# Rotation tables a layer early, a norm on VectorE alone, and other buffer counts in a two-block transformer kernel on one core

## The chip, the cores and the metric

The kernel runs on one core of a Trainium2 chip. The metric is the device time of one execution in microseconds (us), as the median of several runs. In the profile PE is TensorE's matmul stream and PEld its weight loads, DVE is VectorE, ACT is ScalarE, POOL is GpSimd, and SP (SyncE) issues most of the DMAs.

## The reference

The input is one sequence of 512 tokens of width 1024. The first block is two hybrid layers, each a mixer (sparse attention, gated linear attention, pooling) and a convolutional gated feed-forward part, and it ends with a norm. The second block has four layers that run over 256 context tokens and the 512 latent tokens; each is a gated mixer on a normalised and modulated stream, without a feed-forward part. Layers 0 and 3 are of kind 0 (grouped-query attention with axial rotation), layer 1 is of kind 1 (neighbourhood attention) and layer 2 of kind 2 (differential attention, with rotation). What matters here:

```python
# end of the first block: x = rms_norm(x, final_norm_g)

def mixer_a(u, uc, q_g, k_g, ang, need_ctx):       # kind 0
    def heads(t):
        q, k, v = jnp.split(t, [q_dim, q_dim + kv_dim], axis=-1)
        q = rms_norm_2(q.reshape(b, n, A_KV_HEADS, A_GROUP, HEAD_DIM), q_g)
        k = rms_norm_2(k.reshape(b, n, A_KV_HEADS, HEAD_DIM), k_g)
        return q, k, v.reshape(b, n, A_KV_HEADS, HEAD_DIM)
    q, k, v = heads(u)
    qc, kc, vc = heads(uc)
    q, k = axial_rope(q, ang), axial_rope(k, ang)
    o = gqa_attention(q, jnp.concatenate([kc, k], axis=1), jnp.concatenate([vc, v], axis=1))
    ...

def _rotate(x, ang):
    x1, x2 = jnp.split(x, 2, axis=-1)
    ...
    return jnp.concatenate([x1 * cos - x2 * sin, x2 * cos + x1 * sin], axis=-1)
```

The gains q_g and k_g can be multiplied into the cosines and sines, since they depend on the layer and the head's element only. That product is what the kernel calls the rotation tables.

## The kernel before

All products that need float32 precision are made of float16 pairs: a value is split into a high half (ACT casts it) and a low half (POOL or DVE subtracts), and three matmuls add hi by hi, lo by hi and hi by lo. Projections run in units of 128 output columns and two tiles of 128 tokens: 48 matmuls of 128x256 fill one of the two PSUM banks named pj (lines 1609 to 1611). The weights come by DMA as wst and are split into whi (line 376) and wlo (line 377).

The program is a set of Python generators, one for projections and one for attention, that yield after each piece of work. A timeline scheduler then sets the final order of the instructions of each engine by estimated times, and places tiles. So a small edit moves instructions far away from it. Each engine runs its own list in order; POOL also issues the small loads of constants, SP the weight loads and the transposing DMAs.

At the seam of the blocks `first_norm` makes the row scales of the final norm as a PSUM tile px (named bx in the trace). From it `make_h` makes the first layer's normalised stream hh and hl (for the latents) without waiting for x itself; then `scale` multiplies x by px and the gain in place, for the eight pieces of 128 channels.

`mixer(i)` runs one layer of the second block. It loads gains and rotation angles (POOL's DMA queue) and makes the tables rc2 and rs2 on POOL. Then follow the jobs of the heads. A job fills the u tile (128 tokens x 6 token tiles x 128 columns) from pj by ACT (line 1626), squares it, and reduces the squares on DVE (line 1629). Together with a query's columns the gate's columns sz are made from the same bank: ACT's tanh (1792) and DVE's product (1793), which is the bank's last reader; for a key it is the value's remainder vl (1691). When u is full, POOL makes the inverse root qny (421), DVE scales u by it (1658), `rope` makes four products f with rs2 (1651) and one with rc2 (1653) on POOL and adds them on DVE (1654). A query then goes through `put_query`: ACT casts it to qst, POOL makes the remainder (1668), SP transposes it to qs. A key goes through `put_key` with the two tiles kst and klt in the same way (1681, 1682, 1685).

Attention takes scores S from PSUM, DVE finds the negative maximum nm (698), ACT makes P by the exponential (701), ACT casts P to hl (717), POOL makes the remainder (718), SP transposes hl to pt, and PE multiplies with the values (728 to 730). The tiles hl, kst and klt of kind 0 share a ring of four buffers (tag phl). The result of a head pair is split into ohl by ACT (1811) and DVE (1812), and a transposing DMA brings it to og, the left operand of the output projection in `out_pair` (392 to 394 are its matmuls).

Of the kernel before, what the change touches and what calls it, by code (L numbers as in the profile page):

```python
# [8 lines left out]
F32 = mybir.dt.float32  # L9
F16 = mybir.dt.float16  # L10
# [3 lines left out]
OP = mybir.AluOpType  # L14
# [4 lines left out]
S = 512  # L19
# [10 lines left out]
GK = 32.0  # L30
# [187 lines left out]
class Kern:  # L218
# [205 lines left out]
    def setup(self):  # L424
        nc, I, const = self.nc, self.I, self.const
# [30 lines left out]
        self.mod = const.tile([128, 4, 24, 2], F32, name="mod")  # L456
        self.adas = self.ada()
        self.nada = self.nmod = 0

# [216 lines left out]
    def expo(self, su, q, segs, mask=None, bias=None, add=None):  # L676
# [14 lines left out]
        p = self.pp.tile([128, self.wide], F32, name="P", tag="P", bufs=self.nbuf[0])  # L691
        nm = self.sm.tile([128, 1], F32, name="nm")
        if bias is None:
# [8 lines left out]
        else:  # L702
            mx = self.sm.tile([128, 1], F32, name="mx")
            nc.vector.tensor_reduce(mx, s[:, 256:512], axis=AX.X, op=OP.min)
            nc.vector.tensor_tensor_reduce(out=p[:, :256], in0=s[:, :256], in1=bias, op0=OP.add, op1=OP.min,
                                           scale=1.0, scalar=mx, accum_out=nm)
            s2 = self.sm.tile([128, 2], F32, name="su2")
            nc.scalar.activation(p[:, :256], p[:, :256], AF.Exp, bias=nm, scale=-1.0, accum_out=s2[:, 0:1])
# [90 lines left out]
    def mixers1(self, l):  # L799
# [144 lines left out]
        def attn(c, qs, kh, kl, vh, vl):  # L944
            for t in range(4):
# [3 lines left out]
                for h in range(2):  # L949
# [4 lines left out]
                    def second(t=t, h=h, pt=pt, su=su):  # L954
# [5 lines left out]
                        if h:  # L960
                            ri = self.sm.tile([128, 2], F32, name="ri")
                            nc.vector.reciprocal(ri, su)
# [331 lines left out]
    def context(self):  # L1294
# [23 lines left out]
        self.lam()  # L1318
        yield True
        self.norm_h(acc, self.vec, CTX, 1.0)  # L1320
        for _ in range(8):
            yield True

    def first_norm(self, accs):
# [4 lines left out]
        a = self.sm.tile([128, 8], F32, name="ag")  # L1329
        nc.vector.tensor_tensor(a, self.vec[0][:, 0], g, op=OP.mult)  # L1330

        def chain(ms):
# [19 lines left out]
            def scale():  # L1352
                for c in range(KD):
                    t = self.f()
                    nc.vector.tensor_scalar(t, px, g[:, c:c + 1], 1.0 / GK, op0=OP.mult, op1=OP.mult)
                    nc.gpsimd.tensor_tensor(self.x[:, c], self.x[:, c], t, op=OP.mult)
                self.dump("xf", self.x)
# [98 lines left out]
    def spare(self, limit):  # L1456

        while self.nada < limit:
            next(self.adas, None)
            yield True  # L1460

    def mixer(self, i):
        nc, I = self.nc, self.I
        kind, j, need = i % 3, i // 3, i < 3
        with ExitStack() as es:
            self.pl = self.pool("pl", 2, es=es)
            pl = self.pl
            G = self.vec[2]
            gv = pl.tile([128, 4, 64], F32, name="gv", bufs=1) if kind == 1 else self.f(256).rearrange("p (a d) -> p a d", a=4)
            nc.gpsimd.dma_start(gv.rearrange("p a d -> p (a d)"), I["gqk"][i:i + 1].to_broadcast([128, 256]))  # L1470
            if kind != 1:

                self.rc2 = pl.tile([128, 2, 6, 64], F32, name="rc2", bufs=1)
                self.rs2 = pl.tile([128, 2, 4, 64], F32, name="rs2", bufs=1)
                rot = self.f().rearrange("p (a t d) -> p a t d", a=2, t=4)
                nc.gpsimd.dma_start(rot, I["rot"].rearrange("p (a t d) -> p a t d", a=2, t=4))
                for t, r, g in ((self.rc2[:, :, 0:4], rot[:, 0], 0), (self.rs2, rot[:, 1], 2)):
                    nc.gpsimd.tensor_tensor(t, r.unsqueeze(1).to_broadcast([128, 2, 4, 64]),
                                            gv[:, g:g + 2].unsqueeze(2).to_broadcast([128, 2, 4, 64]), op=OP.mult)
                nc.gpsimd.tensor_copy(self.rc2[:, :, 4:6], gv[:, 0:2].unsqueeze(2).to_broadcast([128, 2, 2, 64]))  # L1480
            else:
                self.bm = pl.tile([128, 4, 4, 8], F32, name="bm", bufs=1)
                nc.gpsimd.dma_start(self.bm, I["bm"].rearrange("p (j m c) -> p j m c", j=4, m=4))
                self.gg2 = gv[:, 0]
                nc.vector.scalar_tensor_tensor(gv[:, 0], gv[:, 0], -0.125, gv[:, 1], op0=OP.mult, op1=OP.mult)
# [72 lines left out]
    def out_pair(self, p, G, need, i):  # L1558
# [11 lines left out]
        if final and need:  # L1570
            v = self.vec = self.vectors(i + 1)
            self.ready = set()
        for n in ((CTX,) if need else ()) + ((LAT0, LAT1) if final else (LAT,)):
            while final and self.done[n] < 8:
# [42 lines left out]
    def heads(self, n4, then):  # L1617
# [4 lines left out]
        def done(ps, t):  # L1622
            if not got:
                got.extend((self.pl.tile([128, 6, 128], F32, name="u", bufs=2), self.sm.tile([128, 6, 2], F32, name="qss", bufs=4)))
            u, ss = got[:2]
# [35 lines left out]
    def put_query(self, u, n4, qs):  # L1661

        nc = self.nc
        st = self.pl.tile([128, 2, 6, 2, 64], F16, name="qst", tag="stg", bufs=(1,2,2)[self.kind])[:, :, :n4]
        s = st.rearrange("p h t e d -> p t h e d")
# [132 lines left out]
    def attn_group(self, i, kind, g, need, st):  # L1798
# [7 lines left out]
        def put_og(os, t):  # L1806

            if g < (6,6,6,0)[i]:
                for k, o in enumerate(os):
                    v = pl.tile([128, 256], F16, name="ohl", bufs=2)  # L1810
                    nc.scalar.activation(v[:, :128], o, AF.Copy, scale=0.5 * WI)
# [49 lines left out]
        for t in tiles:  # L1861
            cs = []
            su = self.sm.tile([128, 2], F32, name="su", bufs=6)
            for h in range(2):
# [29 lines left out]
                if kind != 2:  # L1894
                    pt = self.item(su[:, h:h + 1], q, segs, bias=bias)

                    def second(t=t, h=h, pt=pt, su=su, vb=vb):
                        c = slice(64 * h, 64 * h + 64)
                        if h == 0:
                            self.o = self.psO()[:, :128]  # L1900
                            ri = self.sm.tile([128, 2], F32, name="ri")
                            nc.vector.reciprocal(ri, su)
# [66 lines left out]
```

## Time and profile before

| quantity | us |
|---|---|
| median of three runs (2887.4, 2887.79, 2878.65) | 2887.4 |
| profiled execution | 2885.51 |
| its span, first to last instruction | 2883.7 |
| TensorE matmuls busy | 2609.6 |
| DVE busy | 2027.3 |
| ACT busy | 1633.9 |
| POOL busy | 1528.1 |

Times in the rows count from the first instruction of the profiled execution. The second block begins near 1290; its layers begin near 1290, 1690, 2090 and 2590. A timeline row gives start and duration, the engine, the line of the kernel, the operation, the tiles that are written and read, and in square brackets how long the engine was idle before it and what ended that. A window row gives for a stretch the busy time of every engine with the count of its instructions, then the mean granted TensorE clock (1.00 is 2.4 GHz, 0.50 is 1.2 GHz), the share of the DMA engines and their rate.

### The profile page before, as it was taken

Reading aid. Unit: us, or ns where it says so; the run is one execution under the profiler, and the core shown is the slowest. Engines: PE = TensorE matmul, PEld = TensorE weight load, DVE = VectorE, ACT = ScalarE, POOL = GpSimd, SP = SyncE. Lnnn points to the kernel's source line nnn. Section 1 sums busy time; section 2 is a strip of 40 time slices with the busy share of each in tenths; the row PEclk is TensorE's granted clock in tenths of the full one; section 3 lists DMA queues with packets and bytes.
Section 4 is the critical chain, followed back from the end, with each engine's and each line's share of the span. In section 5 each row is a group of like instructions: output and inputs, shape, how many; then the busy total and the mean of one; then the engine's idle time right before and its main releaser. Section 6 shows DMA issues by size and latency. Waiting matters only on the chain. (4 is left out here: it accounts for less than half of the span.)

```text
span 2883.7 us, 58883 instructions
## 1 busy us (share of the span) xinstructions
PE 2609.6 (90%) x22594; PEld 1755.9 (61%) x22604; DVE 2027.3 (70%) x3731; ACT 1633.9 (57%) x3471; POOL 1528.1 (53%) x1341
## 2 busy tenths in 40 slices
PE   7899999999889999998988889999879998978896
PEld 4564444445554444447766678887668786657764
DVE  5966787536966888436767677666668888686775
ACT  6575555335575655333775656665545665455773
POOL 6773222116763432216786647776555555345984
PEclk8999999999999999999999999999999999989999
DMA  4346565333355565332799727887525555423995
GB/s 157 101 105 157 176 198 191 106 104 93 105 126 157 165 205 190 100 105 70 149 165 178 140 77 149 168 167 156 112 62 112 115 119 119 99 61 95 193 188 110
DMA packets 645165, 385.24 MB, mean 134 GB/s; under 512 B 564511, under 2 KB 574545, under 8 KB 644881
## 3 DMA queue, kind: packets, MB, share of 16 engines
q1 hardware_dynamic: 643328, 378.39, 54.7%
q8 instruction: 177, 2.90, 0.4%
q0 software_dynamic: 1120, 2.88, 0.4%
q14 instruction: 108, 0.88, 0.1%
q10 hardware_dynamic: 432, 0.20, 0.0%
HBM read 232.71 MB, written 2.10 MB: 81 GB/s over the span
## 5 line engine op out<-in xcount | busy, mean ns | idle before, releaser
L718 POOL TENSOR_TENSOR hl<-P,hl 128x768 f16<-128x768 f32 (+4 forms) x368 | 463.9, 1267 | 247.9 <-ACT hl L717 205.7
L377 DVE SCALAR_TENSOR_TENSOR wlo<-wst,whi 128x1024 f16<-128x1024 f32 (+1 forms) x292 | 377.6, 1294 | 234.2 <-ACT whi L376 233.1
L1609 PE MATMUL pj<-whi,hh 128*128 128x256 f16 x1664 | 458.0, 276 | 28.1 <-DVE vl L1691 14.3
L1610 PE MATMUL pj<-wlo,hh 128*128 128x256 f16 x1664 | 457.7, 275 | 0.0
L1611 PE MATMUL pj<-whi,hl 128*128 128x256 f16 x1664 | 456.1, 275 | 1.8 <-DVE hl L1452 1.7
L376 ACT ACTIVATE whi<-wst 128x1024 f16<-128x1024 f32 (+1 forms) x292 | 304.4, 1045 | 263.9 <-PE pj L393 149.7
L701 ACT ACTIVATE P<-S,nm 128x768 f32<-128x768 f32 (+4 forms) x352 | 250.9, 715 | 178.0 <-DVE nm L698 91.0
L393 PEld LDWEIGHTS <-whi 128*128 128x128 f16 x1936 | 191.0, 99 | 224.1 <-issue 45.1
L392 PEld LDWEIGHTS <-whi 128*128 128x128 f16 x1936 | 191.3, 99 | 207.6 <-issue 17.1
L394 PEld LDWEIGHTS <-wlo 128*128 128x128 f16 x1936 | 191.1, 99 | 194.9 <-issue 7.2
L717 ACT CAST hl<-P 128x768 f16<-128x768 f32 (+4 forms) x368 | 231.5, 637 | 78.6 <-DMA pt<-hl 45.3
L698 DVE TENSOR_REDUCE nm<-S 128x1 f32<-128x768 f32 (+4 forms) x320 | 236.1, 749 | 48.1 <-PE S L686 34.0
L685 PE MATMUL S<-kh,qs 128*128 128x256 f16 (+3 forms) x672 | 203.0, 310 | 48.2 <-ACT P L701 27.1
L728 PE MATMUL O<-vh,pt 128*128 128x64 f16 (+1 forms) x1472 | 189.5, 200 | 53.7 <-DMA pt<-hl 46.8
L1609 PE MATMUL pj<-whi,mxl 128*128 128x256 f16 x704 | 196.3, 279 | 21.2 <-DVE sz L1793 11.5
L1610 PE MATMUL pj<-wlo,mxl 128*128 128x256 f16 x704 | 196.3, 279 | 1.5 <-DVE wlo L377 1.5
L1611 PE MATMUL pj<-whi,mxl 128*128 128x256 f16 x704 | 195.0, 278 | 1.8 <-DVE mxl L1452 1.8
L686 PE MATMUL S<-kl,qs 128*128 128x256 f16 (+3 forms) x672 | 193.7, 311 | 0.0
L421 POOL TENSOR_TENSOR qny<-qss,mhalf 128x12 f32<-128x12 f32 (+1 forms) x52 | 130.2, 2504 | 118.9 <-DVE qss L1635 114.3
L728 PEld LDWEIGHTS <-pt 128*128 128x128 f16 x1536 | 143.5, 99 | 75.7 <-DMA pt<-hl 66.6
L729 PE MATMUL O<-vl,pt 128*128 128x64 f16 (+1 forms) x1472 | 188.7, 200 | 0.0
L730 PE MATMUL O<-vh,pt 128*128 128x64 f16 (+1 forms) x1472 | 188.1, 200 | 0.0
(398 smaller groups left out, 7697.1 us busy)
## 6 DMA issues: line engine op xcount, KB each, us to landing
wst<-i_wts SPq DMA_DIRECT2D x318, 512.0 KB
ast<-i_ada_w SPq DMA_DIRECT2D x96, 512.0 KB
wst<-i_wts SPq DMA_DIRECT2D x16, 384.0 KB
pt<-hl SPq DMA_TRANSPOSE x368
rpb<-i_rpb SPq DMA_DIRECT2D x8, 384.0 KB
xin<-i_x SPq DMA_DIRECT2D x4, 512.0 KB
kh<-h SPq DMA_DIRECT2D x32, 64.0 KB
kl<-h SPq DMA_DIRECT2D x32, 64.0 KB
```

The source lines that it names most:

```text
L376: nc.scalar.activation(hi[:, :n], st[:, :n], AF.Copy, scale=s)
L377: nc.vector.scalar_tensor_tensor(lo[:, :n], st[:, :n], s, hi[:, :n], op0=OP.mult, op1=OP.subtract)
L685: nc.tensor.matmul(d, q, kh, start=True, stop=False)
L686: last = nc.tensor.matmul(d, q, kl, start=False, stop=(mask is None))
L698: nc.vector.tensor_reduce(nm, s[:, :w], axis=AX.X, op=OP.max, negate=True)
L701: nc.scalar.activation(p[:, :w], s[:, :w], AF.Exp, bias=nm, scale=-1.0 if neg else 1.0, accum_out=su)
L717: nc.scalar.copy(hl[:, :w], p[:, :w])
L718: nc.gpsimd.tensor_tensor(hl[:, w:2 * w], p[:, :w], hl[:, :w], op=OP.subtract)
L728: nc.tensor.matmul(o, pt[:, i], vh, start=(i == 0), stop=False)
L1609: nc.tensor.matmul(d, hh[:, k, s], hi[:, k % 4], start=(k == 0), stop=False)
L1610: nc.tensor.matmul(d, hh[:, k, s], lo[:, k % 4], start=False, stop=False)
L1611: nc.tensor.matmul(d, hl[:, k, s], hi[:, k % 4], start=False, stop=(k == KD - 1))
```

## The change

- The tables rc2 and rs2 become tiles that live through the second block. A new function `tables(i)` loads gains and angles and makes them: for layer 0 within the context generator, which runs beside the last feed-forward part of the first block; for layers 2 and 3 in the final `out_pair` of the layer before. `mixer` itself only loads what kind 1 needs.
- In `first_norm`, `scale` was eight DVE products into a temporary and eight POOL products into x. Now it is eight DVE instructions that read px, a scaled gain gs and x, and write x.
- Buffers: u has 3 instead of 2 in kind 0. nm, mx, su2 and ri have 4 instead of 2. ohl has 4 instead of 2. qst, which in kind 0 had one buffer of its own (tag stg), now takes one of the ring of four (tag phl); in kinds 1 and 2 it stays where it was.
- The space for descriptors of POOL's DMAs is 1024 instead of 2048 bytes a partition.

```diff
@@ __init__
+        self.rc2 = const.tile([128, 2, 6, 64], F32, name="rc2")
+        self.rs2 = const.tile([128, 2, 4, 64], F32, name="rs2")
@@ expo (the same for mx, su2; ri in two more places)
-        nm = self.sm.tile([128, 1], F32, name="nm")
+        nm = self.sm.tile([128, 1], F32, name="nm", bufs=4)
@@ context
+        self.tables(0, self.pf)
+        yield True
@@ first_norm
+        gs = self.sm.tile([128, 8], F32, name="gs", bufs=1)
+        nc.vector.tensor_scalar_mul(gs, g, 1.0 / GK)
...
-                    t = self.f()
-                    nc.vector.tensor_scalar(t, px, g[:, c:c + 1], 1.0 / GK, op0=OP.mult, op1=OP.mult)
-                    nc.gpsimd.tensor_tensor(self.x[:, c], self.x[:, c], t, op=OP.mult)
+                    nc.vector.scalar_tensor_tensor(self.x[:, c], px, gs[:, c:c + 1], self.x[:, c], op0=OP.mult, op1=OP.mult)
@@ new
+    def tables(self, i, tmp=None):
+        nc, I = self.nc, self.I
+        gv, rot = (tmp.tile([128, n], F32, name=f"rt{n}", bufs=1) for n in (256, S)) if tmp else (self.f(256), self.f())
+        gv = gv.rearrange("p (a d) -> p a d", a=4)
+        nc.gpsimd.dma_start(gv.rearrange("p a d -> p (a d)"), I["gqk"][i:i + 1].to_broadcast([128, 256]))
+        rot = rot.rearrange("p (a t d) -> p a t d", a=2, t=4)
+        nc.gpsimd.dma_start(rot, I["rot"].rearrange("p (a t d) -> p a t d", a=2, t=4))
+        for t, r, g in ((self.rc2[:, :, 0:4], rot[:, 0], 0), (self.rs2, rot[:, 1], 2)):
+            nc.gpsimd.tensor_tensor(t, r.unsqueeze(1).to_broadcast([128, 2, 4, 64]),
+                                    gv[:, g:g + 2].unsqueeze(2).to_broadcast([128, 2, 4, 64]), op=OP.mult)
+        nc.gpsimd.tensor_copy(self.rc2[:, :, 4:6], gv[:, 0:2].unsqueeze(2).to_broadcast([128, 2, 2, 64]))
@@ mixer: these lines go (kind 1 keeps its own load of gv)
-            if kind != 1:
-                self.rc2 = pl.tile([128, 2, 6, 64], F32, name="rc2", bufs=1)
-                self.rs2 = pl.tile([128, 2, 4, 64], F32, name="rs2", bufs=1)
-                rot = self.f().rearrange("p (a t d) -> p a t d", a=2, t=4)
...
@@ out_pair
             self.ready = set()
+            if (i + 1) % 3 != 1:
+                self.tables(i + 1)
@@ heads
-                got.extend((self.pl.tile([128, 6, 128], F32, name="u", bufs=2), ...
+                got.extend((self.pl.tile([128, 6, 128], F32, name="u", bufs=(3,2,2)[self.kind]), ...
@@ put_query
-        st = self.pl.tile([128, 2, 6, 2, 64], F16, name="qst", tag="stg", bufs=(1,2,2)[self.kind])[:, :, :n4]
+        st = self.pl.tile([128, 2, 6, 2, 64], F16, name="qst", tag=self.kst[0][1], bufs=self.kst[0][2])[:, :, :n4]
@@ put_og
-                    v = pl.tile([128, 256], F16, name="ohl", bufs=2)
+                    v = pl.tile([128, 256], F16, name="ohl", bufs=4)
@@ build
-    nc = _bacc.Bacc("TRN2", target_bir_lowering=False, num_devices=1, dynamic_dma_scratch_size=2048)
+    nc = _bacc.Bacc("TRN2", target_bir_lowering=False, num_devices=1, dynamic_dma_scratch_size=1024)
```

Since the scheduler works by estimated times, the order changes with it. In the changed kernel line numbers are higher by 2 to 9: 1651, 1653 and 1654 become 1660, 1662 and 1663; 1658 becomes 1667; 1682 and 1685 become 1691 and 1694; 1793 becomes 1802; 1668 becomes 1677.

POOL at the start of layer 0, before (x is the residual stream, hl beside hh the low half of the layer's input, qny the inverse root, f and u the rotation, klt a key's remainder):

```order
L1356 TENSOR_TENSOR x<-x,f 128x512
L1449 TENSOR_TENSOR hl<-f,hh 128x256
L1356 TENSOR_TENSOR x<-x,f 128x512 x7
L1476 DMA f<-i_rot 128x512
L421 TENSOR_TENSOR qny<-qss,mhalf 128x12
L1478 TENSOR_TENSOR rc_13919<-f,fs 128x2x256
L1478 TENSOR_TENSOR rs_13920<-f,fs 128x512
L1651 TENSOR_TENSOR f<-u,rs_13920 128x4x2x16 x4
L421 TENSOR_TENSOR qny<-qss,mhalf 128x12
L1653 TENSOR_TENSOR u<-u,rc_13919 128x768
L1651 TENSOR_TENSOR f<-u,rs_13920 128x4x2x16 x4
L1682 TENSOR_TENSOR klt<-u,kst 128x6x2x64
```

and POOL at the same place in the changed kernel:

```order
L1453 TENSOR_TENSOR hl<-f,hh 128x256 x8
L421 TENSOR_TENSOR qny<-qss,mhalf 128x12
L1660 TENSOR_TENSOR f<-u,rs_124 128x4x2x16 x4
L1662 TENSOR_TENSOR u<-u,rc_123 128x768
L421 TENSOR_TENSOR qny<-qss,mhalf 128x12
L1691 TENSOR_TENSOR klt<-u,kst 128x6x2x64
L1660 TENSOR_TENSOR f<-u,rs_124 128x4x2x16 x4
L1662 TENSOR_TENSOR u<-u,rc_123 128x768
L1691 TENSOR_TENSOR klt<-u,kst 128x6x2x64
```

The products of x, the load of the angles and the two table products have left this place, and the first key's rotation stands ahead of the second qny.

DVE at the start of layer 0, before (u<-u,qny is the scale, u<-u,f the rotation's sum, kst and klt the copies within a key's tiles, sz the gate's product that empties a pj bank):

```order
L1635 TENSOR_SCALAR qss<-qss 128x12
L1658 TENSOR_TENSOR u<-u,qny 128x768
L1654 TENSOR_TENSOR u<-u,f 128x512
L1685 COPY kst<-kst 128x12x64
L1685 COPY klt<-klt 128x12x64
L1629 TENSOR_REDUCE qss<-sq 128x4
L1793 SCALAR_TENSOR_TENSOR sz<-sz,pj 128x256
L1629 TENSOR_REDUCE qss<-sq 128x4
L1793 SCALAR_TENSOR_TENSOR sz<-sz,pj 128x256
```

and the same engine in the changed kernel:

```order
L1644 TENSOR_SCALAR qss<-qss 128x12
L377 SCALAR_TENSOR_TENSOR wlo<-wst,whi 128x1024
L1663 TENSOR_TENSOR u<-u,f 128x512
L1694 COPY kst<-kst 128x12x64
L1667 TENSOR_TENSOR u<-u,qny 128x768
L1638 TENSOR_REDUCE qss<-sq 128x4
L1802 SCALAR_TENSOR_TENSOR sz<-sz,pj 128x256
L1694 COPY klt<-klt 128x12x64
L1663 TENSOR_TENSOR u<-u,f 128x512
L1638 TENSOR_REDUCE qss<-sq 128x4
L1802 SCALAR_TENSOR_TENSOR sz<-sz,pj 128x256
```

The first sz stands behind the second key's scale as before, but no longer behind the first key's klt copy.

DVE at the start of layer 3, before:

```order
L1635 TENSOR_SCALAR qss<-qss 128x12
L377 SCALAR_TENSOR_TENSOR wlo<-wst,whi 128x1024
L1658 TENSOR_TENSOR u<-u,qny 128x768
L1654 TENSOR_TENSOR u<-u,f 128x512
L1685 COPY kst<-kst 128x12x64
L377 SCALAR_TENSOR_TENSOR wlo<-wst,whi 128x1024
L1685 COPY klt<-klt 128x12x64
L377 SCALAR_TENSOR_TENSOR wlo<-wst,whi 128x1024
L1629 TENSOR_REDUCE qss<-sq 128x4
L1793 SCALAR_TENSOR_TENSOR sz<-sz,pj 128x256
```

and in the changed kernel:

```order
L1644 TENSOR_SCALAR qss<-qss 128x12
L377 SCALAR_TENSOR_TENSOR wlo<-wst,whi 128x1024
L1638 TENSOR_REDUCE qss<-sq 128x4
L1802 SCALAR_TENSOR_TENSOR sz<-sz,pj 128x256
L1667 TENSOR_TENSOR u<-u,qny 128x768
L1663 TENSOR_TENSOR u<-u,f 128x512
L377 SCALAR_TENSOR_TENSOR wlo<-wst,whi 128x1024
L1694 COPY kst<-kst 128x12x64
L1638 TENSOR_REDUCE qss<-sq 128x4
L1802 SCALAR_TENSOR_TENSOR sz<-sz,pj 128x256
```

Here the first sz has moved ahead of the second key's scale, the rotation's sum and both copies.

POOL at the end of layer 2, with the last query of that layer, before (hl is a remainder of probabilities):

```order
L421 TENSOR_TENSOR qny<-qss,mhalf 128x12
L1651 TENSOR_TENSOR f<-u,rs_27094 128x4x2x16 x4
L1653 TENSOR_TENSOR u<-u,rc_27093 128x768
L1668 TENSOR_TENSOR qst<-u,qst 128x6x2x64
L718 TENSOR_TENSOR hl<-P,hl 128x256
```

and in the changed kernel:

```order
L421 TENSOR_TENSOR qny<-qss,mhalf 128x12
L1660 TENSOR_TENSOR f<-u,rs_124 128x4x2x16 x4
L1473 DMA f<-i_rot 128x512
L1662 TENSOR_TENSOR u<-u,rc_123 128x768
L1475 TENSOR_TENSOR rs_124<-f,fs 128x512
L1475 TENSOR_TENSOR rc_123<-f,fs 128x2x256
L1477 COPY rc_123<-fs 128x2x128
L1677 TENSOR_TENSOR qst<-u,qst 128x6x2x64
L720 TENSOR_TENSOR hl<-P,hl 128x256 x2
```

Layer 3's load of the angles, its two table products and the copy stand ahead of the last query's remainder.

## Rows read from the trace of the kernel before

**Rows 1.** Page, part 1, busy us and share; then the chain's shares by line.
```profile
PE 2609.6 (90%) x22594; PEld 1755.9 (61%) x22604; DVE 2027.3 (70%) x3731; ACT 1633.9 (57%) x3471; POOL 1528.1 (53%) x1341
...
by line: issue 2.7%; DVE nm L698 1.7%; ACT P L701 1.4%; DMA pt<-hl 1.4%; DVE wlo L377 1.1%; POOL qny L421 1.0%; PE pj L392 0.8%; PE pj L393 0.8%; PE pj L394 0.8%; POOL hl L718 0.6%; ACT whi L376 0.6%; POOL f L1651 0.6%; DMA og<-ohl 0.6%; PE
```

**Rows 2.** Windows: start and end, length, busy by engine; layers 0 and 3.
```profile
1345.00:1690.00 345.00, 298.77 (x3278) 231.85 (x3277) 236.66 (x434) 214.77 (x489) 237.31 (x231) 0.97 0.77 147
2655.00:2884.00 229.00, 194.83 (x2288) 146.71 (x2285) 158.70 (x268) 148.60 (x291) 170.72 (x145) 0.97 0.83 161
```

**Rows 3.** Timeline of PE: the first matmul after each long gap.
```profile
1348.45 0.37 PE L1609 MATMUL pj<-whi,mxl 128*128 128x256 f16 x1 [10.19 <-DVE sz L1793]
...
2157.48 0.37 PE L1609 MATMUL pj<-whi,mxl 128*128 128x256 f16 x1 [6.74 <-DVE vl L1691]
...
2641.70 0.39 PE L1609 MATMUL pj<-whi,hh 128*128 128x256 f16 x1 [8.15 <-DVE sz L1793]
```

**Rows 4.** Timeline of ACT at layer 0's start.
```profile
1342.59 0.83 ACT L1681 CAST kst<-u 128x768 f16<-128x768 f32 x1 [12.89 <-DVE u L1654]
1345.80 0.38 ACT L1626 ACTIVATE u<-pj 128x256 f32<-128x256 f32 x1 [2.38 <-POOL klt L1682]
```

**Rows 5.** Timeline of DVE at layer 0's start.
```profile
1318.98 2.15 DVE L1355 TENSOR_SCALAR f<-bx,g 128x512 f32<-128x512 f32 x3
...
1324.48 0.57 DVE L1635 TENSOR_SCALAR qss<-qss 128x12 f32<-128x12 f32 x1
...
1331.02 0.96 DVE L1658 TENSOR_TENSOR u<-u,qny 128x768 f32<-128x768 f32 x1 [2.19 <-POOL qny L421]
...
1339.35 2.55 DVE L1658 TENSOR_TENSOR u<-u,qny 128x768 f32<-128x768 f32 x1 [4.01 <-POOL qny L421]
1341.82 0.68 DVE L1654 TENSOR_TENSOR u<-u,f 128x512 f32<-128x512 f32 x1
...
1347.99 0.41 DVE L1793 SCALAR_TENSOR_TENSOR sz<-sz,pj 128x256 f32<-128x256 f32 x1
```

**Rows 6.** Timeline of POOL at layer 0's start.
```profile
1316.62 10.69 POOL L1356 TENSOR_TENSOR x<-x,f 128x512 f32<-128x512 f32 x7
...
1327.92 3.06 POOL L421 TENSOR_TENSOR qny<-qss,mhalf 128x12 f32<-128x12 f32 x1
1331.15 1.95 POOL L1478 TENSOR_TENSOR rc<-f,fs 128x512 f32<-128x512 f32 x1 [0.17 <-DMA f<-i_rot]
...
1335.39 1.70 POOL L1651 TENSOR_TENSOR f<-u,rs 128x128 f32<-128x128 f32 x4
...
1339.29 1.79 POOL L1653 TENSOR_TENSOR u<-u,rc 128x768 f32<-128x768 f32 x1
```

**Rows 7.** Windows behind the gaps; the last is layer 3's first rotations.
```profile
1348.50:1353.30 4.80, 4.80 (x23) 3.41 (x23) 1.88 (x5) 0.83 (x1) 1.81 (x1) 0.50 0.70 133
2641.70:2647.00 5.30, 5.29 (x25) 3.76 (x26) 3.88 (x8) 0.83 (x1) 3.23 (x2) 0.50 1.05 218
2647.00:2650.00 3.00, 3.00 (x30) 2.68 (x28) 0.33 (x2) 0.22 (x1) 2.78 (x5) 1.00 0.65 125
2625.46:2652.85 27.39, 19.24 (x154) 16.00 (x152) 16.89 (x22) 6.88 (x14) 20.63 (x20) 0.81 0.59 140
```

**Rows 8.** Line 1811 in 2130 to 2590: ACT's waits (us, times); then timelines there.
```profile
  DMA og<-ohl: 14.3, 7
...
2387.73 0.31 ACT L1811 ACTIVATE ohl<-om 128x128 f16<-128x128 f32 x1 [2.27 <-DMA og<-ohl]
...
2388.07 0.29 DVE L1812 SCALAR_TENSOR_TENSOR ohl<-om,ohl 128x128 f16<-128x128 f32 x1 [0.24 <-ACT ohl L1811]
```

**Rows 9.** Line 717 in 1345 to 1690: ACT's waits (us, times).
```profile
  DMA pt<-hl: 11.4, 11
```

**Rows 10.** Timeline of POOL at layer 2's end and layer 3's start.
```profile
2521.39 1.64 POOL L1668 TENSOR_TENSOR qst<-u,qst 128x768 f16<-128x768 f32 x1 [1.87 <-ACT qst L1667]
...
2604.49 1.27 POOL L1478 TENSOR_TENSOR rc<-f,fs 128x512 f32<-128x512 f32 x1
```

More of the change, by code (lines that the diff above doesn't have):

```diff
@@ L702, in expo @@
         else:
-            mx = self.sm.tile([128, 1], F32, name="mx")
+            mx = self.sm.tile([128, 1], F32, name="mx", bufs=4)
             nc.vector.tensor_reduce(mx, s[:, 256:512], axis=AX.X, op=OP.min)
@@ L706, in expo @@
                                            scale=1.0, scalar=mx, accum_out=nm)
-            s2 = self.sm.tile([128, 2], F32, name="su2")
+            s2 = self.sm.tile([128, 2], F32, name="su2", bufs=4)
             nc.scalar.activation(p[:, :256], p[:, :256], AF.Exp, bias=nm, scale=-1.0, accum_out=s2[:, 0:1])
@@ L960, in second @@
                         if h:
-                            ri = self.sm.tile([128, 2], F32, name="ri")
+                            ri = self.sm.tile([128, 2], F32, name="ri", bufs=4)
                             nc.vector.reciprocal(ri, su)
@@ L1468, in mixer @@
             G = self.vec[2]
-            gv = pl.tile([128, 4, 64], F32, name="gv", bufs=1) if kind == 1 else self.f(256).rearrange("p (a d) -> p a d", a=4)
-            nc.gpsimd.dma_start(gv.rearrange("p a d -> p (a d)"), I["gqk"][i:i + 1].to_broadcast([128, 256]))
-            if kind != 1:
-                self.rc2 = pl.tile([128, 2, 6, 64], F32, name="rc2", bufs=1)
-                self.rs2 = pl.tile([128, 2, 4, 64], F32, name="rs2", bufs=1)
-                rot = self.f().rearrange("p (a t d) -> p a t d", a=2, t=4)
[L1476 to L1481, printed above, removed]
+            if kind == 1:
+                gv = pl.tile([128, 4, 64], F32, name="gv", bufs=1)
+                nc.gpsimd.dma_start(gv.rearrange("p a d -> p (a d)"), I["gqk"][i:i + 1].to_broadcast([128, 256]))
                 self.bm = pl.tile([128, 4, 4, 8], F32, name="bm", bufs=1)
@@ L1623, in done @@
             if not got:
-                got.extend((self.pl.tile([128, 6, 128], F32, name="u", bufs=2), self.sm.tile([128, 6, 2], F32, name="qss", bufs=4)))
+                got.extend((self.pl.tile([128, 6, 128], F32, name="u", bufs=(3,2,2)[self.kind]), self.sm.tile([128, 6, 2], F32, name="qss", bufs=4)))
             u, ss = got[:2]
@@ L1900, in second @@
                             self.o = self.psO()[:, :128]
-                            ri = self.sm.tile([128, 2], F32, name="ri")
+                            ri = self.sm.tile([128, 2], F32, name="ri", bufs=4)
                             nc.vector.reciprocal(ri, su)
```

## The prediction

> **What bounds the kernel now.** The page comes first. TensorE (PE) is busy for 90% of the span, and no other engine for more than 70% [rows 1]. So time can only be won where PE stands still or runs slowly, and the next view is the windows by stretch: in the attention of layers 0 and 3 of the second block PE stands still for 345.0 - 298.8 = 46 us and 229.0 - 194.8 = 34 us [rows 2]. The timeline of PE shows the largest single pieces: one gap each at the start of layers 0, 2 and 3, of 10.19, 6.74 and 8.15 us, ended each time by an evacuation on VectorE (DVE) [rows 3]. They begin at 1348.45 - 10.19 = 1338.26, 2150.74 and 2633.55.
>
> Why the evacuation is late is read backwards. The matmul at 1348.45 needs a bank of the "pj" pair; both wait to be read. ScalarE (ACT) should read the first one into a third u tile, but there are two u tiles, and both still hold keys: ACT's read starts at 1345.80, released by GpSimd's (POOL's) klt, the last reader of the first key's u [rows 4]. DVE's sz, which empties the bank, follows at 1347.99 [rows 5]. Layers 2 and 3 have the same release. klt itself is late because POOL is: in layer 0 it multiplies x (10.69 us for the last seven of eight), only then begins qny at 1327.92, makes two tables from 1331.15 on (1.95 us for the first), and comes to the key's first rotation at 1335.39 [rows 6].
>
> Each gap is followed by a slow stretch. The granted clock is 0.50 (the 1.2 GHz level) from 1348.5 to 1353.3 and from 2641.7 to 2647, and 1.00 (2.4 GHz) behind the latter [rows 7]; before both, PE had stood still. Half of 4.8 and of 5.3 us is lost there: 2.4 and 2.6 us.
>
> **Layer 0's start.** The change takes the eight x products and the two tables off POOL's path and gives u a third buffer. qny needs qss, ready at 1324.48 + 0.57 = 1325.05 [rows 5]. From there, with the rows' durations: qny 3.06, to 1328.1; the u scale on DVE 0.96, to 1329.1; four f on POOL 1.70, to 1330.8; u by rc 1.79, to 1332.6; u add 0.7, the key's cast 0.8 [rows 4] and a copy, taken like sz at 0.4, to 1334.5; the second key's qny on POOL meanwhile, again 3.06, to 1335.7, and its scale to 1336.7; the reduction and sz 0.8, to 1337.5. In the new order sz stands behind exactly these. PE's last matmul before the gap ends at 1338.26, so there is no gap, and no drop of clock: 10.2 + 2.4 = 12.6 us on PE. The second sz comes by the same count (klt like u at 1.8, f, u, add, reduction, sz) at 1342.5, while the next group of 48 matmuls (3.0 us for 30) lasts to 1343.1 [rows 7], so nothing new stops PE there. Attention waits for the first query, whose matmuls are on this path, and so starts 12.6 earlier. The eight new x products on DVE (one tensor in PSUM, one in SBUF) have no row of before. The nearest row is the removed product of the same size, 2.15 us for three [rows 5]; from no more than that to twice that, the eight add 0 to 5.7 us. I take 0, since one input is PSUM as there. With the upper end sz comes up to 5.7 later, at 1343.2, and 4.9 of the gap come back: 8 us left. I take **-12**, from -12.6 to -8.
>
> A row shows what may eat into this: DVE's second u scale took 2.55 us instead of 0.96 where POOL's product of u by rc, 1.79 us, had begun 0.06 before it [rows 5, 6]. The Trainium skill, "SBUF — State Buffer", section "Who interferes with whom", states the rule: a DVE instruction with two SBUF inputs contends with a GpSimd instruction that reads SBUF, and whichever issues second waits in full. The trace agrees (2.55 against 0.96). In the new order klt stands on POOL just where DVE has the second scale; by the rule the scale takes 1.6 longer, sz comes at 1339.1, the gap is 0.8 instead of 0, and this term is -11.8 instead of -12.6.
>
> **Layer 3's start.** u has three buffers here too, and sz of the first query now stands ahead of the second key's scale, so PE goes on at 2633.56: 8.15 + 2.6 = 10.8 us on PE. But the first scores wait for the query's rotation on POOL, and POOL is busy for 20.63 of the 27.39 us from the key's rotation to the query's cast remainder [rows 7]: at most 6.8 us go there, and about 5.7 if a wait of 1 us for a scale stays. Attention bound, 5.7; PE bound, 10.8; I take **-7**. The tables here lie in idle time of POOL before and after the change. Layer 2 keeps two u tiles and its gap of 6.74.
>
> **ohl from 2 to 4 buffers.** ACT waits 7 times, 14.3 us in all, in layer 2 for og's transposes to read ohl. The typical row is 2.27 us at 2387.73; but DVE, which comes next, was busy with something else until 2387.82 and waited only 0.24 us for it [rows 8]. The chain has 0.6% for it, 17 us of 2883.7 [rows 1]. So from 0.24 x 6 groups = 1.4 to 17; I take **-4**, near the lower end, since the one row on who waits behind ACT is there.
>
> **qst into the ring of hl.** In layers 0 and 3 the query's tile had a buffer of its own and now takes one of four that keys and probabilities share. Eight queries a layer pass through it, each time leaving three to hl. In layer 0 ACT's hl casts wait already 11 times, 11.4 us in all, for a buffer there, 1.04 us a time [rows 9]. None of it on the path: 0; each of 16 queries one such wait more on the path: 17 us. Most queries are cast in a pause of ACT, so **+2**.
>
> **Tables ahead.** Layer 0's lie in the last feed-forward stretch, layer 2's in an idle hole of POOL at layer 1's start: 0. Layer 3's now stand ahead of layer 2's last qst: twice 1.27 and a copy, some 2.9 us, where POOL waited 1.87 [rows 10], so that qst comes 1.0 to 2.9 later, which costs 0 where other work hides it: **+1**. The smaller norms' buffers (nm, mx, su2, ri): 0, since the scores' two PSUM buffers are released by the same instructions. Small gaps at the other transitions: **-1**. The first block's code is the same, but the scheduler gives some of its casts and loads another order: 0, within 4 either way.
>
> Sum: -12 - 7 - 4 + 2 + 1 - 1 = **-21 us**. The profiled execution took 2885.5 (span 2883.7), 1.9 under the median 2887.4 of the three runs, so 2864.5 by the one and 2866.4 by the other: **2865**.
>
> **The rivals.**
> *Given back:* layers start earlier but attention, with DVE at 70% of the span, runs at its own pace and returns half of the two starts: -21 + 10 = -11, about 2875; nothing else moves it under 0.3% unless ohl is also worth nothing: 2880. For it: PE idles in dozens of small gaps in these stretches. Against: what comes behind is the same work in the same order.
> *ohl on the path:* 17 instead of 4, 2852. For it the chain's share; against it DVE's 0.24.
> *Slower:* qst in the ring of four. If each of the 16 queries holds up hl by 2 us and that is on the path, 32 us, then -21 - 2 + 32 = +9: 2896. It decides against the change from 1.9 us a query on; the waits of today are 1.04 each, and PE's products with the probabilities wait behind those casts.
> *Doesn't do it:* the third u tile frees ACT, but sz is still behind a late DVE instruction (the u add of the first key), so both gaps stay within a few us: -5, 2880.
>
> **How the numbers follow.** Forecast, 2855 to 2873: 0.62. Given back, 2873 to 2880: 0.18. ohl on the path, 2845 to 2855: 0.08. Doesn't do it, 2878 to 2887: 0.06. Slower: 0.06. A measurement tells about 0.3%, 8.7 us: faster is below 2878.7, slower above 2896.1. Faster: 0.62 + 0.08 + two thirds of 0.18 = 0.82, less a little for the unknown order in the first block, 0.80; slower 0.06; the rest 0.14. The range 2848 to 2881 leaves the slower case, most of "doesn't do it" and the far end of ohl out.
>
> **What would show it.** In the new trace: no gap over 2 us on PE near 1338 and 2633 (in that program's own times), clock 1.00 behind them, ACT's u never released by klt in layers 0 and 3, the gap in layer 2 as before; ACT's wait of ohl for og near zero with little change of group time; hl's wait for its buffer not over 20 us in layer 0. Wrong would make it: a new gap on PE after the second key, hl casts waiting at each qst, or a first block that differs by over 4 us.

## The result and the profile after

The changed kernel takes 2901.3 us (median of 6 runs, 2897.3 to 2908.0) against 2886.3 us of the kernel before in the same comparison: a ratio of 1.0052, 95% interval 1.0039 to 1.0065. It is 15 us slower. I had forecast 2865, with 2881 as the upper end.

What I forecast at the start of layers 0 and 3 did happen. The windows of the changed kernel (start and end, length, busy time by engine, granted clock, DMA share and rate) cover layer 0's start, layer 3's start, and layer 3's attention from its first scores to the end; the last line is the timeline of PE at layer 2's start:

```profile
1336.00:1352.00 16.00, 15.66 (x145) 13.88 (x143) 11.30 (x17) 6.76 (x15) 12.54 (x11) 1.00 0.56 157
...
2632.00:2648.00 16.00, 14.56 (x134) 12.90 (x132) 12.95 (x16) 6.39 (x11) 14.05 (x15) 1.00 0.47 115
2655.00:2906.00 251.00, 199.73 (x2230) 145.85 (x2230) 146.82 (x261) 148.59 (x284) 162.63 (x144) 0.93 0.76 145
...
2158.40 0.37 PE L1618 MATMUL pj<-whi,mxl 128*128 128x256 f16 x1 [6.75 <-DVE vl L1700]
```

PE is busy where gaps of 10.19 and 8.15 us stood [rows 3], and the clock is 1.00 where it was 0.50 [rows 7]. Layer 2 keeps its gap. The small loss that the prediction expects from POOL and DVE side by side came too, without a gap on PE: the second key's scale took 2.38 us, where the first took 0.96, and POOL's klt had begun 0.07 us before it. Timelines of POOL and DVE:

```profile
1348.38 1.64 POOL L1691 TENSOR_TENSOR klt<-u,kst 128x768 f16<-128x768 f32 x1
...
1348.45 2.38 DVE L1667 TENSOR_TENSOR u<-u,qny 128x768 f32<-128x768 f32 x1 [0.21 <-POOL qny L421]
```

But layer 3's attention, which took 229 us [rows 2], takes 251, at a mean clock of 0.93 instead of 0.97. PE's waits in that stretch (us in total, times, longest) are

```profile
PE S L687 <- DMA qs<-qst: 15.4, 8, 3.4
PE S L687 <- ACT P L703: 12.0, 15, 1.7
PE O L730 <- DMA pt<-hl: 8.7, 9, 2.1
```

where in the kernel before the first two were

```profile
PE S L685 <- DMA qs<-qst: 1.9, 1, 1.9
PE S L685 <- ACT P L701: 6.6, 10, 1.3
```

(1.9 us, not the 2.8 that the expectation of run e1 names.) The first scores of nearly every head pair now wait for that pair's queries. One query of layer 3 shows why. These lines are from the timelines of DVE, ACT, POOL, SP and PE of the changed kernel:

```profile
2658.12 0.68 DVE L1663 TENSOR_TENSOR u<-u,f 128x512 f32<-128x512 f32 x1
...
2676.87 0.62 ACT L1676 CAST qst<-u 128x512 f16<-128x512 f32 x1 [0.62 <-DMA pt<-hl]
...
2680.61 1.61 POOL L1677 TENSOR_TENSOR qst<-u,qst 128x512 f16<-128x512 f32 x1
...
2682.24 2.79 SPq L1682 DMA_TRANSPOSE qs<-qst  x2
...
2684.98 0.51 PE L687 MATMUL S<-kh,qs 128*128 128x512 f16 x1 [2.23 <-DMA qs<-qst]
```

The query is rotated at 2658.8, and ACT casts it only at 2676.87, 18 us later, behind seven casts of probabilities (hl). ACT hardly waits in front of it: 0.62 us. So it isn't a buffer that holds this cast up at run time; the cast stands late in ACT's order. With the own buffer of run e1 the same query goes from rotation to cast in one microsecond:

```profile
2655.53 0.68 DVE L1664 TENSOR_TENSOR u<-u,f 128x512 f32<-128x512 f32 x1
...
2657.27 0.62 ACT L1677 CAST qst<-u 128x512 f16<-128x512 f32 x1
```

It is the same with the other queries. From the end of the rotation to the start of the cast, layer 3's eight queries take at most 0.7 us in the kernel before and 1.1 in e1; in the changed kernel the first takes 0.1 and the other seven 11 to 40.

Where the rest went is read from the starts of matching matmuls in the two profiled executions. That of the changed kernel, 2908.0 us, was its slowest, 22.5 us of span over the one of before. It is 4.8 us behind after the first mixer of the first block, 10.3 behind at the block's end, and 1.8 behind at layer 0's first scores, so layer 0's start gave 8.5. It is 0.7 ahead at layer 3's first scores and 20.6 behind at layer 3's last.

### The profile page after: what moved, and what is told of

Read it like the earlier page. It is cut to its first block, busy times and chain, and to the rows that moved or that the text cites. A ratio compares the mean times of both kernels' runs of the same rounds, so it can differ in the third digit from the quotient of the medians.

```text
span 2906.2 us, 58840 instructions
## 1 busy us (share of the span) xinstructions
PE 2620.8 (90%) x22604; PEld 1760.7 (61%) x22604; DVE 2011.8 (69%) x3732; ACT 1640.1 (56%) x3471; POOL 1508.3 (52%) x1333
## 5 line engine op out<-in xcount | busy, mean ns | idle before, releaser
L392 PEld LDWEIGHTS <-whi 128*128 128x128 f16 x1936 | 191.4, 99 | 209.7 <-issue 19.6
L394 PEld LDWEIGHTS <-wlo 128*128 128x128 f16 x1936 | 191.3, 99 | 197.3 <-issue 9.7
L730 PE MATMUL O<-vh,pt 128*128 128x64 f16 (+1 forms) x1472 | 193.8, 202 | 47.9 <-DMA pt<-hl 45.1
L732 PE MATMUL O<-vh,pt 128*128 128x64 f16 (+1 forms) x1472 | 192.2, 201 | 0.0
```

What stands on the lines that cost most here:

```text
L392: nc.tensor.matmul(ps, a, u, start=(k == 0), stop=False)
L730: nc.tensor.matmul(o, pt[:, i], vh, start=(i == 0), stop=False)
```

## The experiments

Each run below was compared with runs of the kernel before on the same chip. In the table all times are us; the ratio is to the kernel before, with its 95% interval. "Scores" are the starts of score matmuls (S) in the profiled execution, one of each kernel. How far single executions of one kernel lie apart is seen from e16 and e18, which are the same kernel: 3 us in the last column.

| run | median | ratio | layer 0, first scores | layer 3, first scores | layer 3, first to last |
|---|---|---|---|---|---|
| before | 2886 | | 1373.7 | 2656.2 | 194.5 |
| changed | 2901.3 | 1.0052 (1.0039 to 1.0065) | 1375.5 | 2655.5 | 215.8 |
| e1 changed, qst own in layer 3 | 2885.1 | 0.9999 (0.9984 to 1.0014) | 1378.5 | 2652.9 | 193.0 |
| e2 changed, no gs | 2907.2 | 1.0075 (1.0052 to 1.0098) | 1368.9 | 2653.2 | 215.6 |
| e3 both | 2884.2 | 0.9989 (0.9978 to 1.0000) | 1366.3 | 2651.8 | 199.3 |
| e4 before, qst in the ring | 2917.3 | 1.0104 (1.0083 to 1.0125) | 1372.9 | 2661.7 | 218.8 |
| e5 before, norm on DVE | 2875.0 | 0.9959 (0.9946 to 0.9972) | 1360.2 | 2638.3 | 193.7 |
| e6 e5, third u in layer 3 | 2871.1 | 0.9942 (0.9922 to 0.9961) | 1362.8 | 2638.1 | 194.2 |
| e7 e3, tables by temporaries | 2870.7 | 0.9953 (0.9936 to 0.9969) | 1362.1 | 2640.2 | 197.3 |
| e8 e5, four ohl | 2871.9 | 0.9958 (0.9943 to 0.9974) | 1364.1 | 2641.8 | 191.4 |
| e9 e5 with gs | 2874.9 | 0.9963 (0.9949 to 0.9977) | 1369.1 | 2648.9 | 195.7 |
| e10 e5, tables ahead | 2879.5 | 0.9978 (0.9963 to 0.9992) | 1367.5 | 2648.4 | 193.2 |
| e11 e10 by temporaries | 2873.9 | 0.9959 (0.9944 to 0.9974) | 1363.8 | 2641.4 | 193.7 |
| e12 changed, mended | 2875.4 | 0.9970 (0.9958 to 0.9982) | 1361.8 | 2643.0 | 194.3 |
| e13 e4, ring of five | 2905.4 | 1.0064 (1.0048 to 1.0080) | 1376.7 | 2656.8 | 214.6 |
| e14 changed, u 2, ring of five | 2909.2 | 1.0075 (1.0056 to 1.0095) | 1374.7 | 2647.8 | 218.1 |
| e15 e11, four ohl in layer 2 | 2865.6 | 0.9927 (0.9911 to 0.9943) | 1363.5 | 2634.4 | 193.7 |
| e16, e18 e15, third u in layer 3 | 2863.9, 2860.8 | 0.9918 (0.9899 to 0.9936), 0.9919 (0.9905 to 0.9934) | 1361.7, 1363.4 | 2630.1, 2630.7 | 197.2, 194.0 |
| e17 e16, tables at the layer | 2867.8 | 0.9938 (0.9917 to 0.9960) | 1365.2 | 2637.3 | 194.1 |

**The query's buffer: e1, e4, e13, e14.** e1 changes one tile of the changed kernel in one layer; e4 puts that tile into the ring in the kernel before:

```diff
e1, e3
+            self.qown = i == 3
-        ... name="qst", tag=self.kst[0][1], bufs=self.kst[0][2])
+        ... name="qst", tag="stg" if self.qown else self.kst[0][1], bufs=1 if self.qown else self.kst[0][2])
e4, e13
-        ... name="qst", tag="stg", bufs=(1,2,2)[self.kind])
+        ... name="qst", tag=self.kst[0][1], bufs=self.kst[0][2])
e13, e14
-            ... self.nbuf ... = ((3,4,8),(3,4,8),(4,3,5))[kind]
+            ... self.nbuf ... = ((3,5,8),(3,4,8),(4,3,5))[kind]
e14
-        ... name="u", bufs=(3,2,2)[self.kind])
+        ... name="u", bufs=2)
```

> The changed kernel, but in layer 3 alone the query's tile qst has its own buffer again (tag stg, one buffer), with u still at 3. Theory A (qst in the ring of hl is what costs layer 3 its time: PE waits at each group of heads for qs<-qst, 15.4 us in the stretch, where before has 2.8): from the first scores of layer 3 to the last 195 us as before instead of 215.8, no gap of 8 us at its start, time about 2880 against 2901. Theory B (layer 3 is slow because of the order that three u buffers bring, the ring has no part): the same 215 us, 2900.

> The kernel before with one edit: qst takes a buffer of the ring phl in kind 0 (layers 0 and 3). Theory A: layer 3 alone grows by 20 or more, layer 0 by 0 to 10, so 2906 to 2916 against 2886. Theory B (the ring costs only together with three u buffers): 2884 to 2890.

Theory A holds in both directions: 16 us come back in e1 (2901.3 to 2885.1), 31 are lost in e4 (2886 to 2917). In all kernels of the table layer 3's scores last 191 to 199 us with the own buffer and 215 to 219 with the ring. Layer 0 is less clear: the casts are late there too, by 8 to 20 us for six of eight queries in the changed kernel and 8 to 24 in e4, and layer 0's scores last 10 us longer in e4 (286.6 us against 276.4), but only 2 longer in the changed kernel (278.2). PE's waits in layer 3 of e4 say the same:

```profile
PE S L685 <- DMA qs<-qst: 15.9, 6, 4.6
```

e13 and e14 ask whether a slot is missing or the turn is the matter.

> The kernel e4 (before, qst in the ring of hl in kind 0) with five buffers in that ring instead of four, so that hl has four left when a query holds one. Theory A (a slot is missing): as before, 2884 to 2890 against e4's 2917. Theory B (the query waits for its turn in the ring behind hl of the group before, so that each group begins with PE waiting for qs): still over 2900, qs<-qst waits of PE in layer 3 over 8 us.

> The changed kernel with two u buffers in kind 0 and the freed space as a fifth buffer of the ring. Theory A: layer 3 no longer loses, 2883 to 2888 against 2901. Theory B: 2895 or more.

With a fifth slot, the same space as before, most of the loss stays: 2905 and 2909, theory B. The slot is not worth nothing: e13 is 12 us below e4, with intervals apart, and the scores of layers 0 and 3 are 5 and 4 us shorter. But 19 of 31 us remain. PE's wait in layer 3 of e13:

```profile
PE S L685 <- DMA qs<-qst: 11.1, 4, 3.4
```

So the number of slots is the smaller part. The larger is where the cast stands: in e13 seven of layer 3's eight queries are still cast 8 to 42 us after their rotation (one is rotated at 2703.2 and cast at 2735.09). ACT's order was fixed before the run, and at run time ACT stood idle for 1.1 us in all before these eight casts, so it is the order that makes them late. Why the scheduler orders them so is my reading and not shown, since its own reckoning was not looked at: a tile of a ring is allotted in the order in which the program asks for it, and the query asks in the middle of a head pair's probabilities. In its own buffer its cast can be put ahead of all of them. In the ring it takes a slot that one of them held before it, and its cast is put at that place, up to a head pair later.

**The first norm: e5, and gs: e2, e3, e9.** e5 takes the change's first norm alone into the kernel before, without the small product gs; e9 is e5 with gs. The lines show e2 and e3 against the changed kernel; e5's first norm is that of e2:

```diff
e2, e3 (k=GK is a new argument of bcast, the factor that it puts in)
-            mm, mx = self.bcast(z, 4, ps), self.bcast(y, 4, px)
+            mm, mx = self.bcast(z, 4, ps), self.bcast(y, 4, px, 1.0)
-        gs = self.sm.tile([128, 8], F32, name="gs", bufs=1)
-        nc.vector.tensor_scalar_mul(gs, g, 1.0 / GK)
-                    ...(self.x[:, c], px, gs[:, c:c + 1], ...
+                    ...(self.x[:, c], px, g[:, c:c + 1], ...
```

> The kernel before with the first norm's x products on VectorE alone, without gs (the broadcast leaves the factor 32 out); tables, u, ohl and qst as before. Up to the first norm the order of all instructions is that of before. Theory A (POOL's eight products are the larger part of what makes layer 0's first key late): the gap at layer 0's start shrinks from 10.2 to about 4, no slow clock behind it, 2886 - 8 = 2878. Theory B (the two u buffers hold the gap, whoever multiplies x): gap 8 or more, 2883 to 2887.

e5 gains 11 us, the largest single gain of all parts. Timelines of POOL, DVE, ACT and PE of e5, layer 0's start:

```profile
1322.05 2.30 POOL L421 TENSOR_TENSOR qny<-qss,mhalf 128x12 f32<-128x12 f32 x1 [2.17 <-DVE qss L1633]
...
1334.77 0.38 ACT L1624 ACTIVATE u<-pj 128x256 f32<-128x256 f32 x1 [2.21 <-POOL klt L1680]
...
1336.07 0.41 DVE L1791 SCALAR_TENSOR_TENSOR sz<-sz,pj 128x256 f32<-128x256 f32 x1
...
1336.53 0.27 PE L1607 MATMUL pj<-whi,mxl 128*128 128x256 f16 x1 [0.62 <-DVE sz L1791]
```

ACT still waits for klt, since there are two u buffers, but klt is early enough: the gap is 0.62 instead of 10.19, and the first scores come at 1360.2 instead of 1373.7 (3.3 of that came with the first block). Without the norm's POOL products there is nothing left for the tables to win here: from the first matmul of px (bx in the trace) to layer 0's first scores it is 71.2 us in the kernel before, 62.6 in the changed one, 60.9 in e5, which makes the tables at the layer's start, and 60.9 in e10 and e11, which make them ahead. POOL makes the tables ahead of qny now (1317.39 and 1318.61, not shown), in time that the x products had filled.

> The changed kernel without the small product gs = g / 32: the broadcast of y that makes px leaves the factor 32 out instead, and the eight x products take g itself. Theory A (gs depends only on a constant, so the scheduler puts it among the first VectorE instructions, and this one instruction shifts the order of the whole first block, which is 10 us longer): the first block ends 5 to 10 us earlier than in the changed kernel, time 2891 to 2896. Theory B (the first block is longer because of the smaller descriptor space, or by chance from run to run): 2901.

> Both edits together, the own buffer of qst in layer 3 and no gs. If both theories A hold, the two add up: 2901 - 21 - 8, about 2872, below the kernel before. If one falls, 2880 or 2893; if both, 2901.

> The kernel e5 (before, first norm on VectorE alone) but with the small product gs as the change has it. Theory A (gs is taken to the first microseconds, since its input is a constant, and the order of the whole first block moves with it): the first mixer ends 4 to 7 us later than in e5, 2879 to 2882 against 2875. Theory B (that order is as good as the other, and run e2's gain in the first mixer was chance): 2875.

gs reads a constant only, so the scheduler puts it among the first VectorE instructions of the program, and from there the order of casts and loads in the first mixer differs. In the profiled executions the four kernels with gs that were laid beside before (changed, e1, e9, e14) are 2 to 5 us behind it after that mixer, and those without it from 4 ahead to 1 behind. The medians don't show it: e2 is 6 above the changed kernel, e3 1 below e1, e9 equal to e5. So the place of gs and the new order are shown, a price is not; theory A of e2 and e9 isn't borne out by the time.

**Layer 3's third u buffer: e6.** Besides this edit e6, and e8 and e15 to e18 below, have the change's smaller descriptor space, which pays for the buffers. No run has that space alone.

```diff
+            self.u3 = i == 3
-        ... name="u", bufs=2)
+        ... name="u", bufs=3 if self.u3 else 2)
```

> The kernel e5 with a third u buffer in layer 3 alone, while qst keeps its own buffer (the smaller descriptor space pays for it). Theory A (the gap at layer 3's start is worth its length): gap gone, layer 3's end 7 to 10 us earlier than in e5. Theory B (layer 3's attention sets the pace and gives it back, as run e1 hints, where layer 3 started 9 early and ended 1 early of it): gap gone, end at most 3 us earlier than in e5.

The gap goes (PE's projections run 8 to 10 us ahead of e5 from 2622 to 2634), and the first scores come at 2638.15 instead of 2638.27. Up to 2610 the order of ACT, DVE and POOL is e5's, and e6 is 0.5 us behind e5 just before it, so the descriptor space shows no effect there. Timelines of ACT, POOL and PE in e6:

```profile
2629.84 0.62 ACT L1666 CAST qst<-u 128x512 f16<-128x512 f32 x1 [1.64 <-DVE u L1653]
...
2631.76 2.54 POOL L421 TENSOR_TENSOR qny<-qss,mhalf 128x8 f32<-128x8 f32 x1 [2.68 <-DVE qss L1634]
2634.26 1.15 POOL L1667 TENSOR_TENSOR qst<-u,qst 128x512 f16<-128x512 f32 x1
...
2638.15 0.61 PE L685 MATMUL S<-kh,qs 128*128 128x512 f16 x1 [2.38 <-DMA qs<-qst]
```

The first query is cast at 2630.5, but on POOL its remainder stands behind the second query's qny, which waits 2.68 us for DVE and takes 2.54. Theory B holds in the trace: the last scores differ by 0.3 us. The medians, 2871.1 and 2875.0, have overlapping intervals. The same edit on e15 (e16 and e18 below) brings the first scores 3.5 us forward, and of that 0 (e16) to 3 (e18) are left at the last.

**The tables: e7, e10, e11.** e10 adds the change's tables to e5; e11 (on e10) and e7 (on e3) put the inputs of layer 0's tables into the usual temporaries:

```diff
-        self.tables(0, self.pf)
+        self.tables(0)
```

> The kernel e5 with the tables made ahead as the change has it, layer 0's inputs in tiles of their own (loads start as soon as the second mixer of the first block gives up its space); u, ohl and qst as before. Theory A (the two loads stand beside the last transposes and cost 5 to 8 us there): 2880 to 2884 against 2875. Theory B (tables ahead cost nothing by themselves; the loss was in the company of the other edits): 2872 to 2876.

> The kernel e10 with layer 0's inputs in the usual temporaries, so that the loads start later. Theory A: the stretch around 890 as in e5, the tables out of layer 0's start, 2872 to 2876. Theory B: as e10.

> The kernel e3 (changed kernel, own buffer of qst in layer 3, no gs), with the inputs of layer 0's tables in the usual temporaries, so that their two loads on POOL's queue start some 15 us later and no longer beside the last transposes of the first block's second mixer. Theory A (these loads hold up the last pt<-hl: 7 us from issue to landing instead of 3, then a slow clock): the stretch around 890 is 5 to 6 us shorter than in e3, 2878 against 2884. Theory B (the stretch is longer by the new order of casts): no difference, 2884.

e10 loses 4.5 us against e5 and e11 has them back: one of e10's nine runs lies among e11's five, the others above them. e7 is 13.5 below e3, and in the profiled executions about 6 of it stand in this stretch; the rest was not followed. e10's timelines of POOL, SP and PE near the end of the first block's second mixer:

```profile
885.66 0.63 POOL L1469 DMA_DIRECT2D rt<-i_gqk  x1
886.29 0.54 POOL L1471 DMA_DIRECT2D rt<-i_rot  x1
...
885.74 1.23 SPq L723 DMA_TRANSPOSE pt<-hl  x1
...
895.33 0.24 PE L730 MATMUL O<-vh,pt 128*128 128x64 f16 x1 [5.55 <-DMA pt<-hl]
```

and the windows of that stretch, first in e10, then in e11:

```profile
885.00:925.00 40.00, 31.48 (x159) 14.24 (x157) 25.61 (x29) 18.54 (x28) 20.45 (x16) 0.96 0.74 194
...
885.00:925.00 40.00, 38.82 (x224) 18.30 (x222) 30.80 (x36) 24.41 (x39) 18.43 (x16) 1.00 0.68 211
```

The loads go out beside the mixer's last transpose, PE waits 5.55 us for it, and in 40 us it works 31.5 instead of 38.8. In e11, whose order is the same up to these loads, no PE gap over 0.8 us stands there: from the issue of that transpose to PE's first use it is 5.0 us, in e10 9.6.

**ohl and the parts together: e8, e12, e15 to e18.**

```diff
e8
-                    v = pl.tile([128, 256], F16, name="ohl", bufs=2)
+                    v = pl.tile([128, 256], F16, name="ohl", bufs=4)
e15 (on e11; the others on e15)
+                    v = pl.tile([128, 256], F16, name="ohl", bufs=(2,2,4)[kind])
```

> The kernel e5 with four ohl buffers instead of two (and the smaller descriptor space). My step in the prediction: -4 against e5, with ACT's waits of ohl for og gone. Rival with the chain's share: -17. Rival: 0 to +3, since DVE is busy meanwhile and the order moves.

> The changed kernel with all that the runs speak against undone: qst in its own buffer in layers 0 and 3, two u buffers everywhere, no gs, layer 0's tables by temporaries; four ohl and the other buffers stay. If the parts add up: e5 (2875) less 0 to 3 for ohl, so 2872 to 2875; if tables ahead and ohl are worth what I forecast, 2867.

> The kernel e11 (norm on VectorE alone without gs, tables ahead by temporaries) with four ohl buffers in layer 2 alone and two in layers 0 and 1. If the four are worth what the profiled executions show for layer 2 (3 to 5 us) and nothing is lost in layer 0: 2869 to 2871 against 2873.9. If it is chance: 2874.

> The kernel e15 with a third u buffer in layer 3. By e6's trace the third buffer closes the gap and moves nothing at the end: as e15, within 2 us. If e6's median (4 below e5) was more than chance: 4 less than e15.

> The kernel e16 with the rotation tables made at the start of their layer as in the kernel before: norm on VectorE alone without gs, a third u buffer in layer 3, four ohl in layer 2, the smaller descriptor space. My step in the prediction (tables ahead take POOL's work off layer 0's start): 2868 or more against e16's 2863.9. Rival (tables ahead win nothing there, and cost a few us at layer 2's end): 2859 to 2864.

> The kernel e16 once more on the same chip and beside the same runs as e17: 2863.9 within 3.

e8 is 3 below e5, within the scatter. In its profiled execution it falls back by 10 us within layer 0, near 1540, where the clock falls to 0.76 and PE waits 4.9 us for pt<-hl and 2.1 for split weights, and wins that back later; e12 falls back there by 11 against e11. Both have four ohl buffers and the own buffer of qst in layer 0; I have no single cause for the loss. e12, the changed kernel with everything undone that the runs speak against, takes 2875.4 and so no less than e5: tables ahead and four ohl everywhere win nothing together. With four buffers in layer 2 alone e15 is 8 below e11, more than I expected. Up to layer 2 the two run in the same order and lie within 2 us of each other, and the profiled execution gains 7 between layer 2's first and last scores. The same edit is all that parts e17 from e6: there it is worth 3 by the medians, with overlapping intervals, and 4 in layer 2's scores. What remains of ACT's wait there in e15 (us, times):

```profile
  DMA og<-ohl: 2.6, 2
```

against 14.3 us, 7 times [rows 8]. e16 and e18 are the same kernel, the best of all: 2863.9 and 2860.8, 0.8% below the kernel before. e17 moves the tables back and is 4 to 7 above them, with overlapping intervals; its profiled execution is 3.4 us behind e16's before layer 0 begins and 4.2 at the end. At layer 0's start the tables ahead win nothing (above); whether they win anything elsewhere stays open.

## Why the prediction was wrong, point by point

- *Layer 0's start, -12.* Right in place and about right in size: 8.5 us in the changed kernel, 10.2 in e5 (which came to the layer 3.3 ahead of before). The eight new products take 0.74 us each against 0.72 of those removed, so my zero for them held. Wrong was to whom I gave it: I needed u and tables too, but e5 gets all of it from the norm alone. POOL's 12 us were the delay, and two u buffers were enough once klt was on time.
- *Layer 3's start, -7.* The gap went, the gain didn't come: at the first scores 0.1 us (e6 against e5) or 3.5 (e16 and e18 against e15), at the last between 0 and 3. The step that failed is the lower end of 5.7, made from POOL's idle time. I let the idle time vanish without following the order: the first query's remainder stands behind a qny that waits for the second query. The rival "given back" comes nearest here.
- *ohl, -4.* Mechanism right, and the size as far as it is known: 8 (e15 against e11) or 3 (e17 against e6) by the medians, for layer 2 alone. In the changed kernel itself ACT's wait in layer 2 is down to 1.9 us, but layer 2's scores last 382.5 us against 381.6 before, so no gain is seen there. In layer 0 four buffers rather cost (e8, e12).
- *qst in the ring, +2.* This is the step that made the prediction wrong: it cost 16 us in layer 3 of the changed kernel (e1), and 31 in layers 0 and 3 of e4. I asked only who would wait for a slot of the ring, and a missing slot is the smaller part (12 of 31). hl's waits, which I named as the sign, stayed small: 17.6 us in layer 0 where the bound I gave was 20 and before had 11.4 [rows 9]. I had read in the trace that the query was cast in a pause of ACT, and didn't ask whether it could still be: its place in the order now hangs on the probabilities before it. The rival "slower" had the tile and the layers, at 2896, but the wrong victim: hl doesn't wait for the query, the query stands behind hl. (By that rival's own terms the loss is clear of noise from 2.0 us a query on, not 1.9.) The late casts stand in the order of ACT in the changed kernel, which I didn't follow.
- *Tables ahead, +1.* Wrong in place. I looked at the products on POOL; the loads cost 4.5 us (e10), beside a transpose in the first block, a stretch that I had put at 0.
- *The first block, 0 within 4.* 10.3 us longer in the profiled execution: 4.8 after the first mixer, where gs changes the order, and about 5 more in the stretch of the loads. The former isn't in the medians. A first block that differs by over 4 us was one of my own signs of being wrong.

The sum of what was measured, from the medians: -11 (norm, e5), +4.5 (loads, e10 against e5), and the ring with +31 (e4) make +24, before ohl's part and the third u; the changed kernel shows +15. The parts don't add up exactly, since every edit moves the order of others: the ring costs 16 in the changed kernel's layer 3, and in its layer 0, where the casts are late too, the scores last only 2 longer.

## What to carry to other kernels

A tile that moves from an own buffer into a shared ring does not only compete for slots: here a scheduler also put its producer behind that of the tiles that were asked for before it. Before sharing, look in the order of the changed kernel how far the producer has moved from the instruction that it follows; one slot more brought back 12 of 31 us. A closed gap of the busiest engine is worth what its next consumer gains, so follow the first consumer's chain instruction by instruction in the new order, and take the edits of a bundle apart: one of them was worth 11 us, and another cost 16 to 31.

## What the runs showed of the hardware

Two loads of 128 and 256 KB on POOL's queue, beside a transposing DMA on SP's, kept PE waiting 5.55 us for the transpose (e10): 9.6 us from its issue to PE's first use, against 5.0 with the loads later (e11). The loads themselves took 5.0 and 8.8 us from issue to landing there:

```profile
rt<-i_rot POOLq DMA_DIRECT2D x1, 256.0 KB, 8.8
rt<-i_gqk POOLq DMA_DIRECT2D x1, 128.0 KB, 5.0
```

A DVE product of a PSUM and an SBUF tensor, 128x512, takes 0.74 us, nearly as long as the same product with one input (0.72 [rows 5]).
